# The odd layer's out projection: three quarters by seven block products, mixers as the stationary operand, residual token-major

## The chip, the cores and the metric

One Trainium2 chip; the kernel runs on one core. The metric is the device time of one execution in microseconds (us), median of the runs shown; the profile is one execution taken by the hardware profiler.

## What is computed

A trunk of two residual layers over 16 meta tokens and 256 tokens, width 2048. The odd layer (16 heads, 256 mixer channels a head) is differential attention, gated, with an out projection of 4096 by 2048, and the final norm follows:

```python
def odd_mixer(h, w_in, w_out, lam_vecs, c_norm, layer_idx):
    z = jnp.einsum('bld,de->ble', h, w_in)
    cq, ck, cv, cg = split_cols(z, (C_WIDTH, C_WIDTH, C_WIDTH, C_WIDTH))
    ...
    o = diff_attention(q, k, v, lam)
    o = rms_norm(o, c_norm) * (1.0 - lam_init)
    o = o.transpose(0, 2, 1, 3).reshape(Bn, L, C_WIDTH) * jax.nn.silu(cg)
    return jnp.einsum('ble,ed->bld', o, w_out)
...
h = h + odd_mixer(rms_norm(h, norm_c[i]), w_in_c[i], w_out_c[i], diff_lambda[i], diff_norm[i], layer)
return rms_norm(h, final_norm)[:, N_META:]
```

## The kernel before

Every large product is made of three TensorE products: each float32 operand is split into a high part (rounded to fp32r by a copy on ScalarE, L290) and a low part (the difference, on VectorE, L291); high by high, high by low and low by high are summed in PSUM.

Weights come in units of 128 x 2048 floats (1 MB): SyncE loads one into a ring of three buffers (`wr`, L301), `half` splits each half of 1024 columns into `wh` and `wl`, which are rings of four buffers each (`ws`). `run` (L313) walks a plan of units and prepares one unit ahead of the one it multiplies. A projection unit of the odd layer is 48 products into one of three `pj` banks, with the 128 x 128 weight blocks stationary and the 256 or 272 tokens moving; `out_unit` (L716) is twice 24 products and adds each result to the transposed residual `hT` (L725).

A head of the odd layer is eight projection units (q, q, k, k, v, v, g, g), and its attention (`scores_c`, `chain_c`) is started as generators that are stepped once in every 16 products (`product`, L281). Scores go into the two `sc` banks, transposes and the norm's sums into the two `tr` banks, the head's output into the `o` bank. `chain_c` ends by splitting the head's 256 channels into the mixer tiles `mh` and `ml` (L910, L912).

Four heads make a quarter of the 4096 mixer channels. From head 4 on, two out units of the quarter before stand at the end of each head (L926): 24 units for three quarters. The last quarter is multiplied in `final` with the mixers stationary and 512 weight columns moving; there the residual is first transposed into token-major `ht` (32 transposes, L942, and eight copies, L943), added up and normalized.

The order of instructions on each engine is made by a scheduler that lists the whole program by its own estimate of times; the order in the text of the kernel gives the dependences.

Of the kernel before, what the change touches and what calls it, by code (L numbers as in the profile page):

```python
# [16 lines left out]
P = 128  # L17
# [13 lines left out]
LAM_INIT = 0.8 - 0.6 * math.exp(-0.3)  # L31
BIG = -1e30
LEV = (1, 2, 4, 8, 16, 32, 64)
DIAG = len(LEV)
# [66 lines left out]
class Trunk:  # L101
# [39 lines left out]
    def setup(self):  # L141
# [37 lines left out]
        nc.vector.memset(self.kT, 0.0)  # L179
        self.qT = c.tile([P, 3 * NM + T], F32, tag="qT", name="qT")  # L180
        self.ones = c.tile([P, P], F32, tag="ones", name="ones")
        nc.vector.memset(self.ones, 1.0)
        nc.vector.tensor_copy(self.onesr, self.ones)

# [96 lines left out]
    def product(self, *args, **kw):  # L281
        if self.products == 16:
            self.products = 0
            self.tick()
        self.nc.tensor.matmul(*args, **kw)  # L285
        self.products += 1


# [19 lines left out]
    def weights(self, src, pieces=1):  # L308

        raw = self.load(src, pieces)  # L310
        return [self.half(raw, 0), self.half(raw, 1)]

    def run(self, plan):  # L313

        srcs = [u for u in plan if isinstance(u, tuple)]
        ready = {}

        def prepare(i):
            if i < len(srcs) and i not in ready:
                ready[i] = self.weights(srcs[i][0], 1 if i else 2)  # L320
# [130 lines left out]
    def chain_a(self, s, mix, slot):  # L451
# [5 lines left out]

        MT = self.one("X3", [3, L])

# [25 lines left out]
        def operands(m):  # L485
            n = (L if m <= 8 else T) // (2 * m)
            w = n * 2 * m
            i = LEV.index(m)
            KS, QS = self.one(f"ks{i % 4}", [L]), self.one(f"u{i % 2}_{i // 2 % 2}", [L])
            for dst, src in ((KS, K), (QS, Q)):  # L490
                nc.scalar.copy(  # L491
                    dst[:, :w].rearrange("p (b d m) -> p b d m", d=2, m=m), view(src, 0, [[2 * m, n], [L + m, 2], [1, m]])
                )
            if m <= 8:
                nc.gpsimd.tensor_copy(self.kT[:, 32 * i - 32 : 32 * i - 32 + NM], KS[:, T:L])
                nc.gpsimd.tensor_copy(self.qT[:, i * NM - NM : i * NM], QS[:, T:L])
            return KS, QS
# [40 lines left out]
        QT = self.two("gate", [NM])  # L538
        nc.vector.tensor_scalar(self.qT[:, 3 * NM + P :], Q[:, 0, :P], tots[:, 1, 1:2], None, op0=ALU.mult)
# [3 lines left out]
        nc.gpsimd.tensor_copy(self.qT[:, 3 * NM : 3 * NM + P], Q[:, 0, P:T])  # L543
        yield
# [7 lines left out]
        W = P + NM  # L552
        mm(tail[:, : 3 * NM + T], lhsT=self.kT, rhs=self.qT, start=True, stop=True)
        mm(xp[:, W + P : 2 * W], lhsT=K[:, 0, P:T], rhs=QT, start=True, stop=True)
# [161 lines left out]
    def out_unit(self, w, key, u, lo=0):  # L716
# [10 lines left out]
        return w[key[1] * 8 + u], products  # L727

    def in_units(self, w, base, begin, lows):
# [73 lines left out]

    def head_c(self, h, mix, slot):
        nc = self.nc
# [33 lines left out]
        def gate(j):  # L839
            def done(ps):  # L840
                if j == 0:
                    s["g"] = self.one("gC", [2, T])
                self.silu(s["g"][:, j], self.scaled(self.two("zg", [T]), ps, NM), T)
                nc.gpsimd.tensor_scalar(s["g"][:, j], s["g"][:, j], self.dn[:, j : j + 1], None, op0=ALU.mult)
                if j == 1:
                    self.start(self.chain_c(s, mix, slot))

            return done
# [3 lines left out]
    def scores_c(self, h, s):  # L852
# [37 lines left out]

    def chain_c(self, s, mix, slot):
        nc, v, wT, gC = self.nc, s["v"], s["w"], s["g"]
# [15 lines left out]
        for j in range(2):  # L908
            nc.gpsimd.tensor_tensor(gC[:, j], gC[:, j], r[:, :T], op=ALU.mult)
        nc.vector.tensor_tensor(gC, o.rearrange("p (a b) -> p a b", a=2), gC, op=ALU.mult)  # L910
        for j in range(2):
            self.split(mix[0][:, slot + j, :T], mix[1][:, slot + j, :T], gC[:, j])  # L912

    def odd(self):
        w_in, w_out = self.ins["w_in_c"], self.ins["w_out_c"]

        def head(h):
            if h % 4 == 0:
                self.mix[1, h // 4] = self.new_mix()
            return self.head_c(h, self.mix[1, h // 4], (h % 4) * 2)  # L920

        plan = [self.setup_odd, lambda: self.stats(self.prenorm(self.gc))]
        for h in range(HC):
            plan += self.in_units(w_in, 8 * h, lambda h=h: head(h), [NM, NM, 0, 0, 0, 0, NM, NM])
            if h >= 4:
                plan += [self.out_unit(w_out, (1, h // 4 - 1), (h % 4) * 2 + u, NM) for u in range(2)]  # L926
        return plan


    def final(self):  # L930
        nc, w, mix = self.nc, self.ins["w_out_c"], self.mix[1, 3]
        fb = self.big.tile([P, D], F32, tag="hl", name="fnorm")
        nc.sync.dma_start(fb, self.ins["fnorm"].broadcast_to([P, D]))
        ht = self.big.tile([P, 2, D], F32, tag="hh", name="ht")
        ms = self.const.tile([P, 2, 5], F32, tag="fms", name="fms")
        rs = self.const.tile([P, 2], F32, tag="frs", name="frs")
        for c in range(4):
            for t in range(2):
                ps = self.ps("tr")
                for e in range(4):  # L940
                    x = self.hT[:, 4 * c + e, NM + t * P : NM + t * P + P]
                    nc.tensor.transpose(ps[:, e * P : e * P + P], x, self.ident)  # L942
                nc.scalar.copy(ht[:, t, c * 512 : c * 512 + 512], ps)  # L943

        def part(ps, t, k, hi, lo, cols=slice(0, 512)):
            ts = slice(t * P, t * P + P)
            for i in range(2):
                s = slice(i * 512 + cols.start, i * 512 + cols.stop)
                kk = 2 * k + i
                last = self.three(ps[:, cols], (mix[0][:, kk, ts], mix[1][:, kk, ts]), (hi[:, s], lo[:, s]), kk == 0, kk == 7)  # L950
            return last
# [54 lines left out]
def layout(inputs):  # L1006
# [12 lines left out]
    w = f["w_out_c"][0]  # L1019
    w3 = w[: 24 * P].reshape(3, 8, P, 8, 2, P).transpose(0, 3, 2, 4, 1, 5).reshape(24, P, 2048)  # L1020
    w1 = w[24 * P :].reshape(2, 4, P, 4, 512).transpose(3, 0, 2, 1, 4).reshape(8, P, 2048)
# [32 lines left out]
```

## Time and profile before

| | |
|---|---|
| median of 3 runs | 2095.29 us (2094.68 to 2095.52) |
| the profiled execution's own time | 2095.99 us |
| its span, first to last instruction | 2094.2 us |
| TensorE busy | 2077.2 us (99%) |
| VectorE / ScalarE / GpSimd busy | 1383.5 / 1162.2 / 585.2 us (66 / 55 / 28%) |
| mean granted TensorE clock | 0.997 |

TensorE issues one instruction after the other and is the engine to look at first; the other engines prepare its operands and empty its banks. Products overlap in the pipeline, so the pace of TensorE is read from the distance between starts, not from the duration of one product.

### The profile page before, as it was taken

The page shows a single profiled execution, that of the slowest core. Times are in us where ns is not written, and L with a number is a line of the kernel's source. Part 1 is how long each engine was busy: PE and PEld are TensorE (multiplying, and loading weights), DVE is VectorE, ACT ScalarE, POOL GpSimd, SP SyncE. Part 2 cuts the span into 40 slices and gives each one's busy share as a digit, 9 for nine tenths or more (in the row PEclk, how much of TensorE's full clock was granted, in tenths as well). Part 3 has the DMA queues.
Part 4 walks back from the last instruction along what each step waited for, and adds up shares of the span by engine and source line. Part 5 has one row for each costly group of instructions (what it writes and reads, how often), then busy time and mean ns, then how long its engine had stood idle before and what let it go on. Part 6 is the DMA issues. An engine that isn't in the chain of part 4 may idle for free.

```text
span 2094.2 us, 40530 instructions
## 1 busy us (share of the span) xinstructions
PE 2077.2 (99%) x16552; PEld 2054.6 (98%) x16552; DVE 1383.5 (66%) x2440; ACT 1162.2 (55%) x2079; POOL 585.2 (28%) x631
## 2 busy tenths in 40 slices
PE   8999999999999999999999999999999999999998
PEld 8999999999999999999999999999999999999997
DVE  7888787877786666656675666665655665655654
ACT  6677666666654545445455555555445555445554
POOL 3453534433442120221022222222122222122211
PEclk9999999999999999999999999999999999999999
DMA  7344443443444444444554444444444444444453
GB/s 269 123 141 148 152 143 142 158 145 142 161 143 161 143 160 155 160 149 151 177 174 168 162 161 162 165 168 172 163 174 168 164 166 174 163 172 171 163 185 116
DMA packets 49146, 336.73 MB, mean 161 GB/s; under 512 B 5568, under 2 KB 5568, under 8 KB 9280
## 3 DMA queue, kind: packets, MB, share of 16 engines
q1 hardware_dynamic: 48240, 333.05, 45.0%
q8 instruction: 130, 2.13, 0.4%
q10 hardware_dynamic: 720, 1.09, 0.2%
q14 instruction: 56, 0.46, 0.1%
HBM read 332.03 MB, written 2.10 MB: 160 GB/s over the span
## 4 chain that ended last, share of the span: by engine, by line
PE 97%; DVE 1%; ACT 1%; issue 0%; DMA 0%; POOL 0%; SPq 0%; DVEq 0%; POOLq 0%; ACTq 0%
PE pspj L285 84%; PE pssc L502 2%; PE pstr L368 1%; PE pso L336 1%; PE pso L335 1%; PE pso L334 1%; PE pspj L334 1%; PE pspj L335 1%; PE pspj L336 1%; PE pssc L336 1%; PE pssc L334 1%; PE pssc L335 1%; PE pssc L514 1%; PE pstr L696 1%; PE pstr L887 1%; DVE wl L291 0%
## 5 line engine op out<-in xcount | busy, mean ns | idle before, releaser
L285 PE MATMUL pspj<-hl,wh 128*128 128x272 f32 (+1 forms) x3936 | 1010.5, 289 | 0.0
L285 PE MATMUL pspj<-hh,wh 128*128 128x272 f32 (+1 forms) x3936 | 1007.5, 287 | 0.0
L290 ACT CAST wh<-wr 128x1024 fp32r<-128x1024 f32 (+1 forms) x628 | 655.0, 1043 | 595.3 <-PE pspj L285 528.3
L291 DVE TENSOR_TENSOR wl<-wr,wh 128x1024 fp32r<-128x1024 f32 (+1 forms) x628 | 774.0, 1233 | 248.9 <-ACT wh L290 246.4
L285 PEld LDWEIGHTS pspj<-hl,wh 128*128 128x128 f32 x3936 | 743.0, 189 | 1.6
L285 PEld LDWEIGHTS pspj<-hh,wh 128*128 128x128 f32 x3936 | 741.1, 188 | 0.7
L285 PE MATMUL pspj<-hh,wl 128*128 128x272 f32 (+1 forms) x3936 | 573.7, 287 | 0.0
L285 PEld LDWEIGHTS pspj<-hh,wl 128*128 128x128 f32 x3936 | 519.7, 189 | 0.9
L285 PE MATMUL pspj<-mh,wh 128*128 128x272 f32 (+1 forms) x896 | 229.5, 288 | 0.0
L285 PE MATMUL pspj<-ml,wh 128*128 128x272 f32 (+1 forms) x896 | 228.9, 287 | 0.0
L285 PEld LDWEIGHTS pspj<-mh,wh 128*128 128x128 f32 x896 | 168.8, 188 | 0.5
L285 PEld LDWEIGHTS pspj<-ml,wh 128*128 128x128 f32 x896 | 169.2, 189 | 0.1
L291 POOL TENSOR_TENSOR X<-z,X 128x256 fp32r<-128x256 f32 (+1 forms) x64 | 77.1, 1206 | 325.4 <-ACT X L290 325.4
L355 DVE TENSOR_TENSOR z<-pspj,rstd 128x272 f32<-128x272 f32 (+1 forms) x114 | 49.6, 436 | 161.5 <-PE pspj L285 161.5
L725 DVE TENSOR_TENSOR hT<-hT,pspj 128x272 f32<-128x272 f32 (+1 forms) x112 | 48.1, 430 | 128.5 <-PE pspj L285 128.4
L285 PE MATMUL pspj<-mh,wl 128*128 128x272 f32 (+1 forms) x896 | 127.8, 285 | 0.0
L285 PEld LDWEIGHTS pspj<-mh,wl 128*128 128x128 f32 x896 | 116.7, 189 | 0.1
L592 POOL TENSOR_TENSOR gC<-sg,zg 128x256 f32<-128x256 f32 x32 | 23.5, 735 | 229.2 <-ACT sg L591 229.2
L856 POOL TENSOR_SCALAR X<-cf 128x272 f32<-128x272 f32 x32 | 43.4, 1365 | 117.6 <-DVE nmx L867 113.9
L423 POOL TENSOR_SCALAR X<-X,lb,lb 128x272 f32<-128x272 f32 x32 | 29.2, 911 | 131.3 <-ACT X L420 121.8
L491 ACT COPY u<-X 128x272 f32<-128x272 f32 (+1 forms) x96 | 40.1, 418 | 45.3 <-DVE X L477 43.8
L463 DVE COPY_PREDICATED X<-masks,pssc 128x256 f32<-128x256 uint8 x128 | 56.5, 441 | 2.3 <-PE pssc L502 1.7
(218 smaller groups left out, 2351.5 us busy)
## 6 DMA issues: line engine op xcount, KB each, us to landing
wr<-in_w_in_c_dram SPq DMA_DIRECT2D x128, 1024.0 KB, 4.8
wr<-in_w_in_a_dram SPq DMA_DIRECT2D x117, 1024.0 KB, 4.8
wr<-in_w_out_a_dram SPq DMA_DIRECT2D x32, 1024.0 KB, 4.9
wr<-in_w_out_c_dram SPq DMA_DIRECT2D x32, 1024.0 KB, 4.8
hT<-in_hT_dram SPq DMA_DIRECT2D x8, 272.0 KB, 6.1
wr<-in_w_in_a_dram SPq DMA_DIRECT2D x8, 256.0 KB, 6.0
wr<-in_w_in_a_dram SPq DMA_DIRECT2D x2, 512.0 KB, 6.7
fnorm<-in_fnorm_dram SPq DMA_DIRECT2D x1, 1024.0 KB, 4.6
```

Source lines behind the costliest of these rows:

```text
L285: self.nc.tensor.matmul(*args, **kw)
L290: self.nc.scalar.copy(hi, src)
L291: (low or self.nc.vector).tensor_tensor(lo, src, hi.bitcast(F32), op=ALU.subtract)
L334: mm(ps, lhsT=a[0], rhs=b[0], start=first, stop=False)
L335: mm(ps, lhsT=a[0], rhs=b[1], start=False, stop=False)
L336: return mm(ps, lhsT=a[1], rhs=b[0], start=False, stop=last)
L355: self.nc.vector.tensor_tensor(dst, ps[:, : L - lo_tok], self.rstd[:, lo_tok:], op=ALU.mult)
L463: nc.vector.copy_predicated(dst, self.masks[:, i, :].unsqueeze(1).broadcast_to([P, 2, P]), src)
L491: nc.scalar.copy(dst[:, :w].rearrange("p (b d m) -> p b d m", d=2, m=m), view(src, 0, [[2 * m, n], [L + m, 2], [1, m]]))
L502: last = mm(lp[:, c], lhsT=KS[:, c], rhs=QS[:, c], start=True, stop=True)
L725: self.nc.vector.tensor_tensor(d, d, ps[:, :n], op=ALU.add)
L856: nc.gpsimd.tensor_scalar(bias[:, i, :], self.negC[i], SLOPES[h] * RS, None, op0=ALU.mult)
```

## The change

For the first three quarters the out projection is made in `group`, in four groups of 512 output columns a quarter. The tokens (two blocks of 128), the quarter's channels (two blocks of 512) and the group's columns (two blocks of 256) form 2 x 2 blocks, and seven block products replace eight. A group takes two weight units, and of each `sums` makes four stationary-side partners on the weight side: one half as it is, two sums of 1024 columns together, one sum of 512, and one half that is partly a sum; all are split into high and low. The mixers are stationary (128 channels x 128 tokens), 256 weight columns move: 84 products a group. The products collect in two `pj` banks (`12`, `34`) and two `sc` banks (`57`, `6`) and are added to the residual at the group's end.

`chain_c` writes the mixers and, for the second two heads of a quarter, four differences of them, into fixed places (`side`). The residual is made token-major once, in the first head of the odd layer (`token_major_residual`), instead of in `final`. The four groups of a quarter stand at the end of heads 4, 8 and 12, after the second k unit and at the end of heads 5, 9 and 13, and after the second k unit of heads 6, 10 and 14. Scores use the `tr` banks. Some buffers of the even layer share places (`ks`, `qT`, `ones`) to make room for `ht`.

```diff
+    def sums(self, src):
+        raw = self.load(src)
+        t = self.spare[:, : 3 * 512]
+        a = self.half(raw, 1)
+        nc.vector.tensor_tensor(
+            t[:, :1024].rearrange("p (a b) -> p a b", a=2),
+            raw[:, :512].unsqueeze(1).broadcast_to([P, 2, 512]),
+            raw[:, 1024:].rearrange("p (a b) -> p a b", a=2),
+            op=ALU.add,
+        )
+        b = self.half(t, 0)
+        nc.vector.tensor_tensor(t[:, 1024:], t[:, :512], raw[:, 1536:], op=ALU.add)
+        c = self.parts()
+        self.split(c[0][:, :512], c[1][:, :512], t[:, 1024:])
+        nc.vector.tensor_tensor(raw[:, :512], t[:, 1024:], raw[:, 512:1024], op=ALU.add)
+        return a, b, c, self.half(raw, 0)
...
+    def group(self, w, q, g):
+        def products(hp, ws):
+            if hp == 0:
+                acc["12"], acc["34"] = self.ps("pj"), self.ps("pj")
+                acc["57"], acc["6"] = self.ps("sc"), self.ps("sc")
+            for part, order in enumerate(
+                ((("X11", "12", 0), ("s3", "34", 0)), (("s1", "57", 0), ("s7", "57", 1)), (("s6", "6", 0),), (("X22", "34", 1), ("X12", "12", 1)))
+            ):
...
+                        for i, (a, b) in enumerate(((xh, wh), (xh, wl), (xl, wh))):
...
+            x = self.two("z", [256])
+            nc.scalar.copy(x, acc["6"][:, :256])
+            nc.vector.tensor_tensor(x, x, p1, op=ALU.subtract)
+            zy = self.spare[:, 3584:4096]
+            nc.vector.tensor_tensor(pair(zy), pair(acc["57"]), x.unsqueeze(1).broadcast_to([P, 2, 256]), op=ALU.add)
...
+            add(h22, acc["57"][:, :256])
+            add(h11, p1)
+            add(h11, p2)
+            add(view(ht, c0 + 256, [[D - 256, 2], [1, 256]]), pair(acc["34"]))
+            add(view(ht, c0 + 256, [[D, 2], [1, 256]]), pair(zy))
+            add(h21, zy[:, 256:], ALU.subtract)
...
-                ps = self.ps("sc")
+                ps = self.ps("tr")
                 c = slice(i * P, i * P + P)
                 self.three(ps[:, :L], (q[:, j, 0, c], q[:, j, 1, c]), (k[:, j, 0], k[:, j, 1]), True, True)
...
-        nc.vector.tensor_tensor(gC, o.rearrange("p (a b) -> p a b", a=2), gC, op=ALU.mult)
-        for j in range(2):
-            self.split(mix[0][:, slot + j, :T], mix[1][:, slot + j, :T], gC[:, j])
...
+        if not half:
+            put("X11", X1[:, :, :P])
+            return
+        put("X12", X[:, :, :P])
+        put("X22", X[:, :, P:])
+        if q == 3:
+            put("X21", X1[:, :, P:])
+            return
+        S = self.spare[:, 2560:3584].rearrange("p (a b c) -> p a b c", a=4, b=2)
+        for i, a, b in ((0, X1[:, :, P:], X[:, :, P:]), (2, X1[:, :, P:], X1[:, :, :P]), (1, X1[:, :, :P], S[:, 0]), (3, X[:, :, :P], S[:, 1])):
+            nc.vector.tensor_tensor(S[:, i], a, b, op=ALU.subtract)
+        for i in range(4):
+            put(SIDES[i], S[:, i])
...
-            if h >= 4:
-                plan += [self.out_unit(w_out, (1, h // 4 - 1), (h % 4) * 2 + u, NM) for u in range(2)]
+            g = {0: [0], 1: [1, 2], 2: [3]}.get(h % 4, []) if h >= 4 else []
+            for i in g:
+                at = 5 if i in (1, 3) else len(units)
+                units[at:at] = self.group(w_out, h // 4 - 1, i)
```

The first place in the order of instructions is VectorE at an out projection. Before, around the two out units that end head 4 (`hT` is the residual, `wl` a low part, `gC` the head's output, `zg` an emptied gate unit):

```order
L355 TENSOR_TENSOR zg_2487_16521<-pspj_2486_16472,rstd_2064_13441 128x256 [waits PE_49]
L291 TENSOR_TENSOR wl_2493_16536<-wr_2489_16529,wh_2492_16535 128x1024 [waits DVE_49,Activation_49]
L725 TENSOR_TENSOR hT_94<-hT_94,pspj_2494_16539 128x256 [waits PE_49]
L291 TENSOR_TENSOR wl_2503_16628<-wr_2501_16625,wh_2502_16627 128x1024 [waits DMAHW5_49,DVE_49,Activation_49]
L725 TENSOR_TENSOR hT_94<-hT_94,pspj_2498_16586 128x256 [waits PE_49]
L291 TENSOR_TENSOR wl_2505_16632<-wr_2501_16625,wh_2504_16631 128x1024 [waits DVE_49,Activation_49]
L725 TENSOR_TENSOR hT_94<-hT_94,pspj_2506_16635 128x256 [waits PE_49]
```

and now, on VectorE at the end of the group that stands inside head 5 (`pspj_2584` is bank `12`, `pspj_2585` bank `34`, `pssc_2586` bank `57`; `u`, `dd`, `nmx` belong to the head's softmax; `wl_2597` to `wl_2614` are the low parts of the two v units that follow):

```order
L967 TENSOR_SCALAR u1_0_2594_17118<-u1_0_2594_17118,dd_2590_17107 128x272 [waits DVE_49]
L291 TENSOR_TENSOR wl_2599_17148<-wr_2595_17141,wh_2598_17147 128x1024 [waits Activation_49]
L968 SCALAR_TENSOR_TENSOR u0_0_2592_17112<-u0_0_2592_17112,dd_2590_17107,u1_0_2594_17118 128x272 [waits DVE_49]
L795 TENSOR_TENSOR ht_13473<-ht_13473,pspj_2585_17072 128x2x256 [waits PE_49]
L792 TENSOR_TENSOR z_2609_17228<-z_2609_17228,pspj_2584_17071 128x256 [waits PE_49,Activation_49]
L795 TENSOR_TENSOR ht_13473<-ht_13473,pspj_2584_17071 128x256
L291 TENSOR_TENSOR wl_2612_17241<-wr_2610_17238,wh_2611_17240 128x1024 [waits DMAHW4_49,Activation_49]
L965 RECIPROCAL dd_2601_17154<-dd_2601_17154 128x2 [waits Activation_49]
L794 TENSOR_TENSOR spare_13681<-pssc_2586_17073,z_2609_17228 128x512 [waits DVE_49]
L795 TENSOR_TENSOR ht_13473<-ht_13473,pssc_2586_17073 128x256
L291 TENSOR_TENSOR wl_2614_17245<-wr_2610_17238,wh_2613_17244 128x1024 [waits Activation_49]
L795 TENSOR_TENSOR ht_13473<-ht_13473,pspj_2584_17071 128x256 [waits DVE_49]
```

The one addition per bank has become a row of steps between the splits for the next units, and the last read of bank `12` comes last of them.

TensorE meets this at the second v unit, whose bank is the one that held `12`:

```order
L286 MATMUL pspj_2615_17248<-hl_2074_13407,wh_2598_17147 128x272
L286 MATMUL pspj_2615_17248<-hh_2073_13406,wl_2599_17148 128x272 x8
L286 MATMUL pspj_2623_17310<-hh_2073_13406,wh_2611_17240 128x272 [waits DVE_49,Activation_49]
L286 MATMUL pspj_2623_17310<-hl_2074_13407,wh_2611_17240 128x272
L286 MATMUL pspj_2623_17310<-hh_2073_13406,wh_2611_17240 128x272
```

The wait on VectorE in the third row is for that last read.

The second place is TensorE after the last projection unit of head 15 (`pso` collects the head's output). Before, an out unit follows between its products:

```order
L336 MATMUL pso_3588_24761<-X3_3559_24549,X4_3551_24519 128x256
L285 MATMUL pspj_3587_24760<-mh_2805_18928,wh_3575_24685 128x256
L285 MATMUL pspj_3587_24760<-ml_2806_18929,wh_3575_24685 128x256
L285 MATMUL pspj_3587_24760<-mh_2805_18928,wh_3575_24685 128x256
L285 MATMUL pspj_3587_24760<-ml_2806_18929,wh_3575_24685 128x256
```

and now the final quarter's products:

```order
L355 MATMUL pso_3719_25174<-X3_3701_24983,X4_3693_24953 128x256
L353 MATMUL pspj_3734_25234<-wh_3725_25216,mh_2083_13460 128x512
L354 MATMUL pspj_3734_25234<-wl_3726_25217,mh_2083_13460 128x512
L355 MATMUL pspj_3734_25234<-wh_3725_25216,ml_2084_13461 128x512
L353 MATMUL pspj_3734_25234<-wh_3725_25216,mh_2083_13460 128x512
```

The two out units that stood behind the last head are gone from there; the products of the final quarter that need the last head's mixers are put behind 56 others that do not.

## Rows read from the trace of the kernel before

**Rows 1.** The page: busy time of TensorE and of the slices, and the chain.
```profile
PE 2077.2 (99%) x16552; PEld 2054.6 (98%) x16552; DVE 1383.5 (66%) x2440; ACT 1162.2 (55%) x2079; POOL 585.2 (28%) x631
...
PE 97%; DVE 1%; ACT 1%; issue 0%; DMA 0%; POOL 0%; SPq 0%; DVEq 0%; POOLq 0%; ACTq 0%
```

**Rows 2.** Windows of the odd layer, then last 8.4 us: busy us (instructions), clock, DMA.
```profile
core 0: us, PE busy (x) PEld busy (x) DVE busy (x) ACT busy (x) POOL busy (x), PEclk, DMA share, GB/s
1125.00:1331.00 206.00, 206.00 (x1697) 205.69 (x1697) 124.76 (x205) 111.55 (x197) 57.80 (x56) 1.00 0.47 164
1345.00:1595.00 250.00, 250.00 (x2070) 249.69 (x2069) 146.20 (x236) 128.58 (x212) 58.40 (x55) 1.00 0.48 167
...
2085.80:2094.20 8.40, 0.28 (x3) 0.08 (x1) 2.12 (x5) 1.73 (x5) 0.00 (x0) 0.64 0.52 178
```

**Rows 3.** Timeline of VectorE (start us, us, what): one step of each head.
```profile
1190.76 0.68 DVE L910 TENSOR_TENSOR gC<-pso,gC 128x512 f32<-128x512 f32 x1
1242.28 0.68 DVE L910 TENSOR_TENSOR gC<-pso,gC 128x512 f32<-128x512 f32 x1
...
1408.22 0.68 DVE L910 TENSOR_TENSOR gC<-pso,gC 128x512 f32<-128x512 f32 x1
1471.11 0.68 DVE L910 TENSOR_TENSOR gC<-pso,gC 128x512 f32<-128x512 f32 x1
```

**Rows 4.** Timeline of TensorE: products with the mixers stationary, 512 and 256 wide.
```profile
2080.02 0.39 PE L336 MATMUL pspj<-wh,ml 128*128 128x512 f32 x1
2080.25 0.28 PE L334 MATMUL pspj<-wh,mh 128*128 128x256 f32 x1
...
2085.80 0.28 PE L336 MATMUL pssc<-wh,ml 128*128 128x256 f32 x1
```

**Rows 5.** Timeline of TensorE: same group of a projection unit, 24 products apart.
```profile
1193.48 1.16 PE L285 MATMUL pspj<-hh,wl 128*128 128x272 f32 x8
1196.50 1.16 PE L285 MATMUL pspj<-hh,wl 128*128 128x272 f32 x8
```

**Rows 6.** The final's transposes, in the chain that ended last.
```profile
2037.97 0.87 PE pstr L942 x8
```

**Rows 7.** Groups of VectorE by form, 1345 to 1845 us (busy us, mean ns, idle before).
```profile
L291 DVE TENSOR_TENSOR wl<-wr,wh 128x1024 fp32r<-128x1024 f32 x160 | 198.5, 1241 | 72.1 <-ACT wh L290 72.1
L725 DVE TENSOR_TENSOR hT<-hT,pspj 128x256 f32<-128x256 f32 x31 | 13.1, 422 | 46.2 <-PE pspj L285 46.2
...
L291 DVE TENSOR_TENSOR X<-pstr,X 128x512 fp32r<-128x512 f32 x8 | 5.5, 684 | 0.0
L910 DVE TENSOR_TENSOR gC<-pso,gC 128x512 f32<-128x512 f32 x8 | 5.4, 678 | 0.0
```

**Rows 8.** The same window on ScalarE.
```profile
L290 ACT CAST wh<-wr 128x1024 fp32r<-128x1024 f32 x159 | 166.9, 1050 | 192.0 <-PE pspj L285 174.3 <-issue 17.7
```

**Rows 9.** Timeline around the last head's chain, all engines but TensorE.
```profile
2027.15 0.60 ACT L901 ACTIVATE X<-pso 128x512 f32<-128x512 f32 x1 [0.61 <-PE pso L899]
...
2029.62 1.22 DVE L291 TENSOR_TENSOR wl<-wr,wh 128x1024 fp32r<-128x1024 f32 x1
2029.77 1.66 POOL L291 TENSOR_TENSOR X<-X,X 128x256 fp32r<-128x256 f32 x1 [0.68 <-ACT X L290]
...
2034.64 1.45 POOL L909 TENSOR_TENSOR gC<-gC,u 128x256 f32<-128x256 f32 x2 [3.21 <-ACT u L391]
...
2035.62 1.54 DVE L291 TENSOR_TENSOR wl<-wr,wh 128x1024 fp32r<-128x1024 f32 x1
...
2039.48 0.75 DVE L291 TENSOR_TENSOR ml<-gC,mh 128x256 fp32r<-128x256 f32 x2
```

**Rows 10.** What TensorE waited for in the whole run (us, times, longest).
```profile
PE pssc L285 <- DVE hl L240: 3.4, 2, 1.8
...
PE pssc L285 <- DVE wl L291: 1.7, 1, 1.7
PE pssc L502 <- DVE X L466: 1.1, 1, 1.1
```

More of the change, by code (lines that the diff above doesn't have):

```diff
@@ L319, in prepare @@
             if i < len(srcs) and i not in ready:
-                ready[i] = self.weights(srcs[i][0], 1 if i else 2)
+                ready[i] = srcs[i][2](srcs[i][0]) if len(srcs[i]) > 2 else self.weights(srcs[i][0], 1 if i else 2)
         i = 0
@@ L456, in chain_a @@
         yield
[L458 removed]
+        MT, qT = self.one("X3", [3, L]), self.one("u_2", [3 * NM + T])
         def keep(i, lp):
@@ L727, in out_unit, with side @@
         return w[key[1] * 8 + u], products
+    def side(self, kind, p, n=1, q=0):
+        b, off = (q % 2, 0) if kind == "X11" else ((q + 1) % 2, 0) if kind == "X21" else divmod(SIDES.index(kind), 3)
+        off = p * P + (0 if kind in ("X11", "X21") else 512 + off * 512)
+        return [x[:, off : off + n * P] for x in self.cm[b]]
+    def group(self, w, q, g):
+        nc, acc = self.nc, {}
+        def products(hp, ws):
[5 more added lines that the diff above has]
+            ):
+                for pr in range(2):
+                    for e, (kind, bank, half) in enumerate(order):
+                        xh, xl = self.side(kind, 2 * hp + pr, 1, q)
+                        e = half if kind in ("s1", "s7") else {"X11": 0, "s3": 1, "s6": 0, "X22": 0, "X12": 1}[kind]
+                        c = slice(e * 512 + pr * 256, e * 512 + pr * 256 + 256)
+                        wh, wl = ws[part][0][:, c], ws[part][1][:, c]
+                        ps = acc[bank][:, half * 256 : half * 256 + 256]
+                        first, last = hp + pr == 0, hp + pr == 2
+                        for i, (a, b) in enumerate(((xh, wh), (xh, wl), (xl, wh))):
+                            start = first and i == 0
+                            with self.tc.issue_after(acc["first" + bank]) if start and half else nullcontext():
+                                ins = self.product(ps, lhsT=a, rhs=b, start=start and not half, stop=last and i == 2, skip_group_check=True)
+                            if start and not half:
+                                acc["first" + bank] = ins.ins
+            if hp == 0:
+                return
+            ht, c0 = self.ht, g * 512
+            p1, p2 = acc["12"][:, :256], acc["12"][:, 256:]
+            pair = lambda x: x.rearrange("p (a b) -> p a b", a=2)
+            x = self.two("z", [256])
[3 more added lines that the diff above has]
+            nc.vector.tensor_tensor(pair(zy), pair(acc["57"]), x.unsqueeze(1).broadcast_to([P, 2, 256]), op=ALU.add)
+            add = lambda d, a, op=ALU.add: nc.vector.tensor_tensor(d, d, a, op=op)
+            h11, h21, h22 = ht[:, 0, c0 : c0 + 256], ht[:, 1, c0 : c0 + 256], ht[:, 1, c0 + 256 : c0 + 512]
+            add(h22, acc["57"][:, :256])
[4 more added lines that the diff above has]
+            add(h21, zy[:, 256:], ALU.subtract)
+        return [(w[(q * 4 + g) * 2 + hp], lambda ws, hp=hp: products(hp, ws), self.sums) for hp in range(2)]
@@ new lines, in token_major_residual @@
+    def token_major_residual(self):
+        nc = self.nc
+        self.ht = self.big.tile([P, 2, D], F32, tag="ht", name="ht")
+        for c in range(4):
+            for t in range(2):
+                yield
+                ps = self.ps("tr")
+                for e in range(4):
+                    x = self.hT[:, 4 * c + e, NM + t * P : NM + t * P + P]
+                    nc.tensor.transpose(ps[:, e * P : e * P + P], x, self.ident)
+                nc.scalar.copy(self.ht[:, t, c * 512 : c * 512 + 512], ps)
+        self.spare = self.big.tile([P, NJ * L], F32, tag="hT", name="spare")
@@ L914, in odd, with first @@
+        for i in range(4):
+            put(SIDES[i], S[:, i])
     def odd(self):
         w_in, w_out = self.ins["w_in_c"], self.ins["w_out_c"]
[L917 to L922, printed above, removed]
-        for h in range(HC):
-            plan += self.in_units(w_in, 8 * h, lambda h=h: head(h), [NM, NM, 0, 0, 0, 0, NM, NM])
-            if h >= 4:
-                plan += [self.out_unit(w_out, (1, h // 4 - 1), (h % 4) * 2 + u, NM) for u in range(2)]
+        def first():
+            self.cm = [self.new_mix() for _ in range(2)]
+            self.cm = [[x.rearrange("p a b -> p (a b)") for x in m] for m in self.cm]
+            self.start(self.token_major_residual())
```

58 lines of the change are left out of this document (33 added, 25 removed).

## Prediction

> **What bounds the kernel.** I read the page first: TensorE is busy 99% of the span and makes 97% of the chain that ended last [rows 1]. The windows then show where that holds: in the odd layer TensorE is busy in every microsecond at full clock, while VectorE has 124.76 of 206 us of work and GpSimd less [rows 2]. The list of waits names the first products of the program and one wait of 1.1 us in the even layer [rows 10]: nowhere in the odd layer does TensorE wait by a measurable amount. So time there is the number of products times the distance between their starts, as long as the other engines stay ahead. The last 8.4 us hold three products [rows 2]; that tail (last additions, norm, stores) is left as it is.
>
> Two prices follow. A head without out units lasts 1242.28 - 1190.76 = 51.52 us, one with two lasts 1471.11 - 1408.22 = 62.89 us [rows 3]: two out units, 96 products, are 11.37 us of pure TensorE time. And products of just the kind the change uses (mixers stationary, 256 columns moving) stand at the end of the program: 48 of them, 47 distances in 2085.80 - 2080.25 = 5.55 us, so 0.1181 us each [rows 4].
>
> **The change, part by part.**
>
> *Products.* Three quarters of eight out units become 12 groups of 84 products. A group costs 84 x 0.1181 = 9.92 us against 11.37: 1.45 us less, 12 times, **-17.4 us**. By 144 products fewer at 0.1181 it would be -17.0. All of it is on the path that sets the end.
>
> *The transposes* leave the final part and enter the first head of the odd layer. Eight took 0.87 us [rows 6], so 32 are 3.5 us, taken away in one full stretch of TensorE and added in another: **0**. Their eight copies on ScalarE run beside a first head in which ScalarE has 111.55 of 206 us of work [rows 2].
>
> *Weight sums and splits.* For one group VectorE has six low parts of 1024 (1.241 us), two of 512 (0.684), two sums of 1024 (taken as a low part, 1.22, [rows 9]), four of 512 (0.678), and at the end five steps of 256 (0.422) and three of 512 [rows 7]: 7.45 + 1.37 + 2.44 + 2.71 + 2.11 + 2.03 = 18.1 us. Two out units had 4 x 1.241 + 4 x 0.422 = 6.7 us. So VectorE gets 11.4 us more in a stretch that gets shorter. Steps that follow each other overlap a little (two low parts of 256, each of the 0.42 us of a step that size, took 0.75 us together [rows 7, 9]: 0.09 us), over some 20 steps 1.8 us, so 16.3 to 18.1 us. The groups stand half a head apart: 51.52 / 2 + 9.92 = 35.7 us of TensorE, in which VectorE has half of a head's 31.2 us (124.76 / 4) and one group: 31.9 to 33.7 us, **89 to 94%** against some 60% now. That still fits, but with 2 to 4 us to spare in each cycle, the attention not evenly spread. ScalarE gets 7.5 casts of 1024 instead of four and a small copy [rows 8], 4 us more on 19 (111.55 / 206 x 35.7) in such a cycle: it has room. The mixers' differences and extra splits (8 subtractions, 6 splits of 256 a quarter) are some 6 us a quarter, spread over heads by the scheduler; in the cycles that have them VectorE comes to 95%.
>
> So I walked through the orders at the group inside head 5, with time 0 at its first product and 0.07 us of overlap taken off each VectorE step. Its last weight part can only be cast when the last part of the unit before is used up, at 5.7; ScalarE is done at 6.75, VectorE at 7.9, TensorE needs it at 10.0: no wait. Then come two score steps (the second can start at 8.6, when TensorE has made it), three splits, the softmax steps and the additions in the order shown; from 9.1 on these are 8.5 us, so bank `12` is free at **17.6**. TensorE is through with the group and the 12 score products between at 11.4, with the next unit (48 at (1196.50 - 1193.48) / 24 = 0.126, [rows 5]) and two transposes at **17.7**, and then needs that bank. That is a tie: without the overlap VectorE is 1.1 us late. The same walk at the group that ends a head (no scores) leaves 1 to 2 us. I take 0.5 us for each of the six groups inside a head and nothing for the others: **+3 us**. The lower end is 0 (TensorE never waits now). The upper is 13 us: all 12 groups late by the 1.1 us.
>
> *The moved load queue.* The weight loads are the same 32; a sum unit holds its buffer until its last split, at 7.9 us after the group's start, and what is loaded into it is first needed at about 18; a load of 10 us would still be in time. Nothing; without that distance the unit two behind would be late.
>
> *The program's end.* The last head's chain loses the two out units that stood behind it. In the trace it takes from 2027.1 to 2040.2, about 13 us [rows 9], with its norm issued late among out products. Now its norm sums stand behind 30 products of 512 at 0.23 us [rows 4], 7 us after the head's last product, and the mixers are ready at 11.4 (high) and 11.9 (low); TensorE has 20 more such products and arrives at 11.9 and 12.4. **+0.5 us**, from 0 to 2.
>
> *Everything else* (shared buffers in the even layer, a memset less, scores in the `tr` banks) changes when steps are issued, not their number. TensorE had no waits there and the even layer's VectorE share does not change: 0, give or take 1 us.
>
> Sum: -17.4 + 3 + 0.5 = -13.9 us. The profiled execution took 2095.99 us, so 2082.1 by it; it lies 0.7 above the median, so I say **2081.5** for the median.
>
> *A rule against the change.* In the trace a low part took 1.54 us instead of 1.22 while GpSimd ran two additions [rows 9], and another GpSimd step took 1.66 us beside a low part. By the Trainium skill (SBUF - State Buffer, "Who interferes with whom") that is what happens when a VectorE step with two SBUF inputs meets a GpSimd step that reads SBUF: one blocks the other for the whole instruction. The trace agrees. All the added sums and splits are such steps; by the mean of the low parts [rows 7] the sum gets nothing for it, and by the rule at every step it becomes the first rival.
>
> **Rivals.**
>
> *The lock makes VectorE the bound (slower).* Of the 18 us a group, some 17 steps have both inputs in SBUF. GpSimd is busy 58.4 of 250 us, 23% [rows 2]. If a meeting costs 0.32 us as in the row, chance meetings are 17 x 0.23 x 0.32 = 1.3 us a group; if every one met and paid it, 5.4 us, and a cycle would need 33.7 + 5.4 = 39 us against 35.7: 3.4 us lost in each, 41 us in all, 2119. It decides from where VectorE's delay passes its slack by 1.45 us a group, which eats the whole gain; at 1.8 us the time is over 2099.5. Against it: the mean low part is 1241 ns beside a bare 1.22 [rows 7, 9], so meetings cost 0.02 us on average. Chance 6%.
>
> *VectorE is late in every cycle.* In-order waits, on scores above all, leave holes in an engine that is 90 to 95% full. At 0.7 to 1.1 us for each of 12 groups: 8 to 13 us lost, 2087 to 2092. For it: the walk's tie; against it: what is late in one cycle is caught up in the four units that follow. Chance 20%; with 1.1 to 1.8 us a group, no measurable change, another 9%.
>
> *The sums don't reach TensorE at all in time, or the products run slower than those at the end.* Two half banks filled in turn are not in the trace; the final part alternates whole banks without a gap. With 0.123 us a product the gain would be 12.5 instead of 17.4, 2086. Chance 5%, inside the range.
>
> **How the numbers follow.** The forecast case (0 to 8 us lost) has 60% and gives 2077 to 2086. With the late cycles and the slower products the range is **2077 to 2092**, which leaves some 15% above and a little below. A measurement of this kernel can tell about 0.2%, 4.2 us. Faster by that is below 2091.1: 60 + 5 + 18 of the late cycles, **0.83**. Within it 0.11; slower 0.06.
>
> **What would show it.** Right: TensorE instructions fewer by 144; group products 0.118 us apart; VectorE busy 130 to 155 us more; TensorE waits in the odd layer few, and those on VectorE steps of the residual (bank `12`) or on low parts, a few us in all; the tail still 8.4 us. Wrong: waits of 1.5 us or more at each group; low parts with a mean well over 1.24 us and GpSimd steps beside them; a gap before the last head's mixers in the final part; or a distance over 0.12 us between group products.

## The result, and the profile after

The changed kernel takes 2081.32 us (median of 4 runs, 2081.09 to 2082.60) against 2095.12 us (4 runs, 2094.68 to 2095.52) of the kernel before on the same chip: 13.8 us less, ratio 0.9935, 95% interval 0.9918 to 0.9953. The prediction was 2081.5. The profiled execution took 2081.48 us, its span is 2079.7 us against 2094.2, 14.5 us less; the terms below are held against that.

The page of the changed kernel: span, busy time, VectorE's 40 slices, and the chain that ended last.

```profile
span 2079.7 us, 40519 instructions
...
PE 2063.0 (99%) x16408; PEld 2039.4 (98%) x16408; DVE 1533.0 (74%) x2650; ACT 1204.0 (58%) x2157; POOL 608.6 (29%) x631
...
DVE  8888887887676656656575666798768896688854
...
PE 92%; DVE 3%; ACT 2%; POOL 1%; issue 1%; DMA 1%; SPq 0%; DVEq 0%; ACTq 0%; POOLq 0%
```

Beside [rows 1]: 144 products fewer (16552 to 16408), VectorE up 149.5 us (1383.5 to 1533.0), and higher slices of VectorE in the last third, where the groups lie. TensorE is still the engine that is always busy.

What TensorE waited for in the whole run of the changed kernel (us in all, times, longest):

```profile
PE pstr L175 <- DVE wS L170: 2.1, 1, 2.1
PE pssc L286 <- DVE hl L240: 2.1, 2, 1.8
PE pssc L286 <- DVE wl L291: 1.7, 1, 1.7
PE pssc L521 <- ACT u L510: 1.0, 2, 0.6
PE pspj L353 <- ACT mh L290: 0.5, 1, 0.5
PE pssc L533 <- POOL X L525: 0.5, 2, 0.3
PE pssc L286 <- ACT hh L239: 0.4, 1, 0.4
```

One line is of the odd layer, the one on `mh`: 0.5 us in the final part, on the last head's mixers. At the twelve groups there is no wait. L521 and L533 are the scan of the even layer, in the first 250 us; beside [rows 10] they are new, or stand in place of the 1.1 us there.

Windows of the changed kernel from the end of one group to the end of the next, three cycles of the first quarter (busy us and instructions of TensorE, its weight loads, VectorE, ScalarE, GpSimd; clock, DMA):

```profile
1348.95:1383.92 34.97, 34.97 (x291) 34.97 (x290) 31.55 (x51) 19.22 (x28) 9.84 (x7) 1.00 0.54 193
1383.92:1420.60 36.68, 36.68 (x306) 36.60 (x305) 32.23 (x46) 23.82 (x41) 9.94 (x10) 1.00 0.48 166
1420.60:1455.53 34.93, 34.93 (x291) 34.93 (x289) 31.72 (x50) 19.20 (x30) 10.14 (x7) 1.00 0.53 186
```

VectorE works 88 to 91% of a cycle, at full TensorE clock and with TensorE busy throughout.

**Where the time went.** The two products on the sink row in each head's attention make a mark. Timeline of TensorE, first mark of heads 0, 3, 7 and 15 in the changed kernel, then of heads 0 and 15 in the kernel before:

```profile
1132.47 0.28 PE L990 MATMUL pso<-wS,vS 80*128 80x256 f32 x1
...
1286.99 0.28 PE L990 MATMUL pso<-wS,vS 80*128 80x256 f32 x1
...
1533.34 0.28 PE L990 MATMUL pso<-wS,vS 80*128 80x256 f32 x1
...
2026.72 0.28 PE L990 MATMUL pso<-wS,vS 80*128 80x256 f32 x1
```

```profile
1128.12 0.28 PE L899 MATMUL pso<-wS,vS 80*128 80x256 f32 x1
...
2025.98 0.28 PE L899 MATMUL pso<-wS,vS 80*128 80x256 f32 x1
```

- Head 0 comes 4.35 us later: about 3.5 us are the 32 transposes, the rest, 0.85 us, is there before the odd layer begins (see the run of the even layer's edits below).
- Four heads with four groups take 1533.34 - 1286.99 = 246.35 us. A head without a group takes 51.51 us in this trace too, so a group costs (246.35 - 4 x 51.51) / 4 = **10.08 us**, 0.1200 us a product, where the prediction had 9.92. Two out units cost 11.37 [rows 3]: 12 x (11.37 - 10.08) = 15.5 us gained, not 17.4.
- From the mark of head 15 to the end: 52.98 us against 68.22, 15.24 less. The two out units that stood there (11.37) and the transposes (3.5) make 14.9 of it; the remaining 0.4 is what three final products ahead of the mark (0.68) and somewhat faster products of 512 columns (below) give, less the wait of 0.5 us and what else moved there.

### The profile page after: what moved, and what is told of

Same layout as the page of the kernel before. It is cut to its first block, busy times and chain, and to the rows that moved or that the text cites. A ratio compares the mean times of both kernels' runs of the same rounds, so it can differ in the third digit from the quotient of the medians.

```text
span 2079.7 us, 40519 instructions
## 1 busy us (share of the span) xinstructions
PE 2063.0 (99%) x16408; PEld 2039.4 (98%) x16408; DVE 1533.0 (74%) x2650; ACT 1204.0 (58%) x2157; POOL 608.6 (29%) x631
## 4 chain that ended last, share of the span: by engine, by line
PE 92%; DVE 3%; ACT 2%; POOL 1%; issue 1%; DMA 1%; SPq 0%; DVEq 0%; ACTq 0%; POOLq 0%
PE pspj L286 78%; PE pssc L286 3%; PE pssc L521 2%; DVE wl L291 1%; PE pstr L387 1%; PE pso L355 1%; PE pso L354 1%; ACT wh L290 1%; PE pso L353 1%; PE pssc L533 1%; DMA wr<-in_w_in_a_dram 1%; PE pspj L353 1%; PE pstr L715 1%; PE pspj L355 1%; PE pspj L354 1%
## 5 line engine op out<-in xcount | busy, mean ns | idle before, releaser
L291 DVE TENSOR_TENSOR wl<-wr,wh 128x1024 fp32r<-128x1024 f32 (+1 forms) x628 | 777.0, 1239 | 217.0 <-ACT wh L290 205.1
L291 POOL TENSOR_TENSOR X<-z,X 128x256 fp32r<-128x256 f32 (+1 forms) x64 | 84.0, 1313 | 256.7 <-ACT X L290 256.7
L286 PE MATMUL pspj<-mh,wh 128*128 128x272 f32 x512 | 135.0, 293 | 0.0
L286 PE MATMUL pspj<-ml,wh 128*128 128x272 f32 x512 | 134.5, 291 | 0.0
L510 ACT COPY u<-X 128x272 f32<-128x272 f32 (+1 forms) x192 | 78.3, 417 | 86.7 <-DVE X L496 50.3
L286 PEld LDWEIGHTS pspj<-mh,wh 128*128 128x128 f32 x512 | 96.3, 188 | 0.5
L286 PEld LDWEIGHTS pspj<-ml,wh 128*128 128x128 f32 x512 | 96.5, 189 | 0.1
L286 PE MATMUL pspj<-mh,wl 128*128 128x272 f32 x512 | 74.8, 288 | 0.0
L744 DVE TENSOR_TENSOR hT<-hT,pspj 128x272 f32<-128x272 f32 x64 | 27.9, 436 | 57.0 <-PE pspj L286 57.0
L286 PEld LDWEIGHTS pspj<-mh,wl 128*128 128x128 f32 x512 | 68.1, 188 | 0.1
```

The costliest lines, as they stand in the source:

```text
L286: return self.nc.tensor.matmul(*args, **kw)
L291: (low or self.nc.vector).tensor_tensor(lo, src, hi.bitcast(F32), op=ALU.subtract)
L510: nc.scalar.copy(dst[:, :w].rearrange("p (b d m) -> p b d m", d=2, m=m), view(src, 0, [[2 * m, n], [L + m, 2], [1, m]]))
```

## The experiments

All times are medians beside the kernel before on the same chip, which took 2094.88 to 2095.26 us. "A quarter" is the distance from the mark of head 3 to that of head 7, four heads with four groups: 246.35 us in the changed kernel.

**Eight products, in the new form.** The groups are kept, without sums; each line of the new table is a mixer block, a bank, its half, and which of the two weight blocks of the part:

```
-    return a, b, c, self.half(raw, 0)
+    return self.half(raw, 1), self.half(raw, 0)
...
-    ((("X11", "12", 0), ("s3", "34", 0)), (("s1", "57", 0), ("s7", "57", 1)), (("s6", "6", 0),), (("X22", "34", 1), ("X12", "12", 1)))
+    (("X11", "1", 0, 0), ("X21", "2", 0, 0), ("X12", "1", 1, 1), ("X22", "2", 1, 1)),
+    (("X12", "1", 0, 1), ("X22", "2", 0, 1), ("X11", "1", 1, 0), ("X21", "2", 1, 0)),
...
```

> The changed kernel with eight plain block products a group in place of seven: mixers stationary, residual token-major, transposes early, as in the change, but no sums of weights, no differences of mixers, and two additions of 512 columns to the residual a group. Theory (TensorE is the bound, VectorE's added steps cost nothing): 144 products more at the 0.120 us that the groups of the changed kernel show, +17.3 us, 2098.6 us (2097 to 2100); a cycle with a group 1.44 us longer. Rival (the seven products' VectorE steps cost TensorE time that no wait shows): less than +16 us.

Measured: 2098.45 us (2098.16 to 2099.91), ratio 1.0017 (1.0008 to 1.0026). A quarter is 252.08 us, a group 11.51, 1.43 more than with seven. The 144 products are worth 17.1 us, and all the sums and differences on VectorE cost TensorE nothing. It also shows that the rest of the change (token-major, mixers stationary) is by itself a loss, 3.6 us: 96 products take 11.51 us this way and took 11.37 in the two out units, 1.7 us over 12 groups. The other 1.9 us were not taken apart; the even layer's edits account for some 0.2 of them (below).

**Where the stationary blocks lie.** Group products stand 0.1200 us apart; the prediction's 0.1181 came from the same kind of product, with the mixers elsewhere in their tile.

```
-    off = p * P + (0 if kind in ("X11", "X21") else 512 + off * 512)
+    off = (p + (0 if kind in ("X11", "X21") else 4 + off * 4)) * 136
...
```

> The changed kernel with its mixer blocks 136 elements apart in place of 128, as blocks of the kernel before lay (272 for two); nothing else. Theory (the distance of 0.120 in place of 0.118 us between group products comes from where the stationary blocks lie): 1008 group products at 0.118, -1.9 us, and the 168 products of 512 columns of the final part back from 0.227 to 0.232 us, +0.8: 2080.2 us, a group 9.92 us. Rival (the distance has another cause): 2081.3, a group 10.08 us.

Measured: 2080.29 us (2079.83 to 2080.80). A quarter is 245.81 us, so a group 9.94. Timeline of TensorE in the changed kernel, and with the stride of 136, two starts 12 products apart in the first group:

```profile
1340.21 0.28 PE L286 MATMUL pssc<-wh,mh 128*128 128x256 f32 x1
...
1341.65 0.28 PE L286 MATMUL pssc<-wh,mh 128*128 128x256 f32 x1
```

```profile
1339.57 0.28 PE L286 MATMUL pssc<-wh,mh 128*128 128x256 f32 x1
...
1340.99 0.28 PE L286 MATMUL pssc<-wh,mh 128*128 128x256 f32 x1
```

1.44 us against 1.42: 0.1200 and 0.1183 each. In the final part the 512 columns went the other way, 0.2275 to 0.2322 on average.

> The changed kernel with all its mixer blocks moved by 8 elements (32 bytes), still 128 elements apart. It tells apart what in the stride mattered. If the place of each block counts (128 elements apart puts every block on a multiple of 512 bytes, 136 apart does not): group products at 0.118, products of 512 columns at 0.232, as with the stride of 136, 2080 to 2081. If the distance between blocks counts: 0.120 and 0.227 as in the changed kernel, 2081.3.

Its edit is `+ 8` at the end of the line that the stride's edit takes out. Measured: 2080.53 us (2080.49 to 2080.69), a quarter 245.90 us, 0.1186 us for 256 columns and 0.2332 us for 512. So the place of each block counts, not the distance between blocks: with every block on a multiple of 512 bytes from the start of its tile, 256 columns take 0.120 and 512 take 0.227; away from it 0.118 to 0.119 and 0.232 to 0.233. Why is not shown. The weight loads of the group products have a mean of 190 to 191 ns in the changed kernel and 188 with the stride of 136, which would fit a longer load; but those of the 512 columns have 188 ns in both, so the length of the load does not explain their distance. By the Trainium skill (TensorE: Matmul & The Clock Gate, "Back-to-back issue gap") the distance in a stream of such pairs is set by the load and the product together; the rows of 256 columns fit, those of 512 show no change of the load, and it says nothing of places.

**The tie at bank `12`.** The prediction's 3 us of waits rest on it. Changed kernel, VectorE's steps on the banks and TensorE around them, after the first group inside head 5 (first product at 1372.49):

```profile
1383.92 0.28 PE L286 MATMUL pspj<-wh,ml 128*128 128x256 f32 x1
1384.04 0.29 PE L286 MATMUL pspj<-hh,wh 128*128 128x272 f32 x1
1385.38 0.67 DVE L795 TENSOR_TENSOR ht<-ht,pspj 128x512 f32<-128x512 f32 x1
1385.97 0.41 DVE L792 TENSOR_TENSOR z<-z,pspj 128x256 f32<-128x256 f32 x1
1386.30 0.41 DVE L795 TENSOR_TENSOR ht<-ht,pspj 128x256 f32<-128x256 f32 x1
...
1389.90 0.40 DVE L795 TENSOR_TENSOR ht<-ht,pspj 128x256 f32<-128x256 f32 x1
1390.29 0.29 PE L286 MATMUL pspj<-hh,wh 128*128 128x272 f32 x1
```

The group ends at 1384.04, 11.55 us after its first product (walked: 11.4). The last read of bank `12` starts at 1389.90 and ends at 1390.30, 17.8 us after the first product (walked: 17.6), and the second unit starts at 1390.29, at 17.80 (walked: 17.7). By the times this looks like the forecast tie, without a wait. To tell a lucky tie from a wrong bank, one step was put in front of that read:

```
     add(h11, p1)
+    add(x, p1)
     add(h11, p2)
```

> The changed kernel with one more VectorE addition of 256 columns (0.41 us, into a scratch tile, the output is the same) before the last read of bank 12 in each group. It also lets one more low part past that read. Theory (the tie of the prediction is real: after the first group inside a head, VectorE's last read of bank 12 ends within 0.1 us of TensorE's need): that read comes about 1.6 us later there, 3 waits of 1.6 us; after the second group inside a head it comes 3.2 us later against a distance of some 2 us, 3 waits of 1.2; none at the ends of heads: +8 us, 2089.5 us, each wait on that addition. Rival (there is slack that the trace does not show, or the next wait is made up): 2081 to 2083.

Measured: 2081.36 us (2081.26 to 2081.53), no change. In this kernel:

```profile
1390.27 0.29 PE L286 MATMUL pspj<-hh,wh 128*128 128x272 f32 x1
1391.14 0.40 DVE L795 TENSOR_TENSOR z<-z,pspj 128x256 f32<-128x256 f32 x1
1391.46 0.41 DVE L795 TENSOR_TENSOR ht<-ht,pspj 128x256 f32<-128x256 f32 x1
```

The unit starts 1.6 us before the last read of bank `12` ends, so it does not write there. The changed kernel's own trace says the same at the group that ends at 1455.53, the second one inside a head:

```profile
1461.92 0.29 PE L286 MATMUL pspj<-hh,wh 128*128 128x272 f32 x1
1462.48 0.41 DVE L795 TENSOR_TENSOR ht<-ht,pspj 128x256 f32<-128x256 f32 x1
```

The second unit starts there 0.97 us before that read ends; it starts ahead of its end, by 0.01 to 0.98 us, after 9 of the 12 groups. So the section on the change has this wrong: the second v unit's bank is not the one that held `12`, and its wait on VectorE in the order is not for that read. The bank of `34` had been read by 1386.05 (the step of 512 at 1385.38 above) and was there to be had. My theory fell; its replacement, that units get whichever bank came free first, was tried with six steps in place of one:

> The changed kernel with six more VectorE additions of 256 columns before the last read of bank 12, which then comes some 20 us after the group. Theory (units are given whichever bank of the three was released first, so two banks carry the units as long as they are read at once, and bank 12 is only missed when the next group wants two, 25 us later): 2081 to 2084. Rival (a unit behind the group does take bank 12 in its turn, with a few us of room): that unit waits more than 10 us in each of 6 groups, over 2140.

Measured: 2081.21 us (2081.00 to 2081.38). The last read now ends at 1404.38, 20.5 us after the group's last product, and TensorE has no wait in the odd layer but the 0.5 us of the final part. In this kernel bank `12` is read 14 us behind the second unit's start and costs nothing: there is no tie. That banks go by the order in which they come free fits all this, but no row names the bank of a unit.

**How full may VectorE be?** Six such steps behind all others, and in the second kernel `range(16)`:

```
     add(h21, zy[:, 256:], ALU.subtract)
+    for _ in range(6):
+        add(x, h21)
```

> The changed kernel with six more VectorE additions of 256 columns a group (some 0.35 us each, 2.1 us a group, 25 us in all, into a scratch tile, the output is the same) behind the last step of the residual, so that bank 12 is not read later. Theory (the amount of VectorE work does not matter while it is not full, only what stands before a step that TensorE needs): VectorE 95 to 98% busy in a cycle with a group, 0 to +3 us, 2081 to 2084. Rival (VectorE is full enough that its work comes through one to one): 1.5 to 2.1 us for each of 12 groups, +18 to +25 us, 2099 to 2106.

Measured: 2081.74 us (2081.02 to 2082.68), a quarter 246.34 us as without them. In the cycles whose windows stand above, VectorE works 34.05 of 34.97, 34.04 of 36.68 and 33.95 of 34.93 us, 93 to 97%, and TensorE does not wait in them.

> The changed kernel with sixteen more VectorE additions of 256 columns a group (0.34 us each, 5.4 us a group) behind the last step of the residual, into a scratch tile. VectorE has 31.97 us of work in a cycle of 35.53 in the changed kernel, so it would have 37.4. Theory (work on VectorE is free up to the length of the cycle and costs one to one beyond it): 1.9 us late in each of the three cycles between the groups of a quarter, made up in the stretch without groups, 9 times 1.9, +17 us, 2098 (2088 to 2105), with waits of TensorE on low parts or on the residual. Rival (the order hides it, the added steps slide behind everything TensorE needs): under 2085.

Measured: 2107.10 us (2105.70 to 2109.35), ratio 1.0057 (1.0042 to 1.0072): slower than before, and 9 us more than forecast. The waits are on what was said (TensorE waited 9.5 us for low parts and 2.3 for casts), with one of 3.0 to 3.2 us in each quarter in place of three of 1.9, but they are not the whole price. Windows of this kernel inside the first quarter (columns as above), the last four of them as one, then one of the changed kernel with about as many products, then TensorE's timeline after the longest wait there:

```profile
1430.00:1435.00 5.00, 5.00 (x43) 5.00 (x43) 4.80 (x7) 2.43 (x4) 3.50 (x1) 1.00 0.57 210
1435.00:1440.00 5.00, 3.88 (x29) 3.46 (x28) 3.86 (x8) 2.03 (x3) 1.10 (x2) 1.00 0.60 210
1440.00:1445.00 5.00, 2.70 (x11) 2.40 (x11) 4.46 (x9) 0.45 (x2) 0.00 (x0) 0.71 0.00 0
1445.00:1450.00 5.00, 4.18 (x17) 3.89 (x18) 4.36 (x11) 1.93 (x3) 1.96 (x1) 0.50 0.00 0
1450.00:1455.00 5.00, 5.00 (x33) 5.00 (x33) 4.90 (x9) 1.82 (x4) 2.11 (x2) 0.77 0.49 165
1435.00:1455.00 20.00, 15.76 (x88) 14.75 (x88) 17.59 (x34) 6.23 (x11) 5.17 (x5) 0.74 0.27 94
```

```profile
1434.00:1445.00 11.00, 11.00 (x90) 11.00 (x90) 9.31 (x12) 4.62 (x7) 2.71 (x2) 1.00 0.28 97
```

```profile
1442.03 0.56 PE L286 MATMUL pssc<-wl,mh 128*128 128x256 f32 x1 [3.01 <-DVE wl L291]
...
1443.24 0.41 PE L286 MATMUL pssc<-wh,mh 128*128 128x256 f32 x1
...
1443.88 0.41 PE L286 MATMUL pssc<-wh,mh 128*128 128x256 f32 x1
```

After a wait of 3.01 us the granted clock is 0.50, 1.2 of 2.4 GHz, and products stand 0.21 us apart ((1443.88 - 1443.24) / 3) in place of 0.12, until it is back at 1.00 some 10 us later. The 88 products of the 20 us from 1435 to 1455 take the changed kernel some 11 us. So 9 us are lost in this stretch: TensorE is idle for 4.24 of them, and the rest goes with the slower products. Here the waits cost their own time and about as much again. The three quarters lost 10.0, 7.8 and 8.4 us against the changed kernel.

**VectorE's steps beside GpSimd's.** Eight GpSimd additions of 256 columns a group, into a scratch tile:

```
     add(h21, zy[:, 256:], ALU.subtract)
+    for i in range(8):
+        nc.gpsimd.tensor_tensor(self.spare[:, 4096:], h21, h11, op=ALU.add)
```

> The changed kernel with eight more GpSimd additions of 256 columns a group into a scratch tile, some 10 us a group: GpSimd 20 us busy in a cycle of 35.5 in place of 9.9. Theory (a meeting of the two engines lengthens the GpSimd step far more than the VectorE step): low parts with a mean below 1.27 us, the GpSimd additions above 1.2 us, 2081 to 2083. Rival (every meeting blocks VectorE for a whole GpSimd step or at the 0.32 us of the row of before): VectorE gets 2 us a cycle or more, is full at 35 us of 35.5, low parts with a mean over 1.35 us beside the groups, 2085 to 2100.

Measured: 2092.03 us (2090.44 to 2092.74), 10.7 us lost: the time and the low parts are those of the rival. Groups of VectorE from 1350 to 1460 us (three groups), by form, in the changed kernel and then in this one, where GpSimd's additions stand in the second row:

```profile
L291 DVE TENSOR_TENSOR wl<-wr,wh 128x1024 fp32r<-128x1024 f32 x37 | 45.7, 1239 | 6.3 <-ACT wh L290 6.3
...
L319 DVE TENSOR_TENSOR spare<-wr 128x1024 f32<-128x1024 f32 x6 | 8.2, 1370 | 0.1
...
L329 DVE TENSOR_TENSOR wr<-spare,wr 128x512 f32<-128x512 f32 x6 | 4.7, 777 | 0.1
```

```profile
L291 DVE TENSOR_TENSOR wl<-wr,wh 128x1024 fp32r<-128x1024 f32 x35 | 47.3, 1354 | 2.3 <-ACT wh L290 2.1
...
L804 POOL TENSOR_TENSOR spare<-ht 128x256 f32<-128x256 f32 x24 | 33.5, 1395 | 13.3 <-DVE ht L795 11.8
L319 DVE TENSOR_TENSOR spare<-wr 128x1024 f32<-128x1024 f32 x6 | 9.3, 1549 | 0.1
...
L329 DVE TENSOR_TENSOR wr<-spare,wr 128x512 f32<-128x512 f32 x6 | 6.2, 1034 | 0.1
```

A low part goes from 1239 to 1354 ns, a sum of 512 from 777 to 1034. Over the forms with two inputs in SBUF (low parts, the three sums, the low parts of sums) that is 35 x 0.115 + 6 x (0.179 + 0.153 + 0.349 + 0.257 + 0.125), some 10 us for 24 GpSimd additions, 0.43 us for each. VectorE then has no room left, 49.49 us of work from 1350 to 1400. The Trainium skill's rule (SBUF - State Buffer, "Who interferes with whom"), that such a pair of steps locks one out, agrees in kind; the trace gives 0.43 us on VectorE for a GpSimd step of 1.4. TensorE's named waits are on GpSimd's split of the score inputs, which stands behind the added steps (4.7 us), and on VectorE (1.6 us): how much of the 10.7 us is the lock and how much that queue, this run does not tell apart, nor that a full VectorE is what sets the time.

**The even layer's edits alone**, on the kernel before:

```
-    nc.vector.memset(self.ones, 1.0)
...
+    self.ones = self.onesr.bitcast(F32)
...
-    MT = self.one("X3", [3, L])
+    MT, qT = self.one("X3", [3, L]), self.one("u_2", [3 * NM + T])
...
-    KS, QS = self.one(f"ks{i % 4}", [L]), self.one(f"u{i % 2}_{i // 2 % 2}", [L])
+    KS, QS = self.one(f"u{2 + i % 2}_{i // 2 % 2}", [L]), self.one(f"u{i % 2}_{i // 2 % 2}", [L])
...
```

> The kernel before with the change's edits of the even layer alone: the scan's key and query buffers under shared tags, the table of ones taken from the other one. Theory (0.8 us of the change's gain is given back there: in the trace of the changed kernel the even layer's products are 0.8 us later from 310 us on, with two new waits of TensorE of 1.0 and 0.5 us in the first 250 us): the same two waits, heads of the odd layer 0.8 us later, 2095.7 us (2095.3 to 2096.3). Rival (those 0.8 us are chance of that execution's start, or come from the odd layer's edits): the head's marks where they were, 2094.9.

Measured: 2096.40 us (2096.25 to 2096.61) against 2095.05, ratio 1.0006 (0.9996 to 1.0015): a little above the range, and not told apart from the kernel before. Its list of waits has the two new ones, and head 0's mark is 0.61 us later than in the kernel before:

```profile
PE pssc L501 <- ACT u L490: 0.9, 2, 0.6
PE pssc L513 <- POOL X L505: 0.5, 2, 0.3
```

But most of that is there before the two waits, the first of which ends at 128 us. The first product on `wS` and `vS` in the even layer, in the kernel before, in this one and in the changed one:

```profile
79.30 0.29 PE L573 MATMUL pso<-wS,vS 80*128 80x272 f32 x1
79.71 0.29 PE L572 MATMUL pso<-wS,vS 80*128 80x272 f32 x1
79.93 0.29 PE L592 MATMUL pso<-wS,vS 80*128 80x272 f32 x1
```

It comes 0.41 us later here and 0.63 us later in the changed kernel. In the profiles of the kernels derived from the changed one it lies between 79.33 and 80.41 us, and head 0's mark between 1131.84 and 1132.92: the program's start varies by that much. From this product to head 0's mark, these edits add 0.20 us. So some 0.2 of the 0.85 us come from them, and some 0.6 from the start of that one execution; the theory's 0.8 us was too much.

**The fastest.** Stride 136 for the three quarters of the groups, 128 for the last one, whose products are 512 wide:

```
+    step = P if q == 3 else 136
+    off = (p + (0 if kind in ("X11", "X21") else 4 + off * 4)) * step
...
```

> The changed kernel with mixer blocks 136 elements apart for the three quarters that the groups use, and 128 apart for the last quarter, which the final part uses. Theory (each width has its better place: 256 columns 0.118 us at the stride of 136, 512 columns 0.227 at that of 128): 1.7 us less in the groups, the final part as in the changed kernel, 2079.6 us (2079.2 to 2080.4), the fastest of all. Rival (the 512 columns' distance does not come from the stationary blocks): 2080.3, as with one stride.

Measured: 2079.46 us (2079.35 to 2081.03), ratio 0.9926 (0.9913 to 0.9940), the fastest of all: a quarter is 245.81 us, 512 columns take 0.2275.

## Why the prediction was right, and where only its sum was

The forecast case came in: TensorE is the bound, and VectorE's added work is hidden. But three terms were off and nearly cancelled, so that 2081.5 came within 0.2 us of the measured time is luck:

| term | predicted, us | measured, us |
|---|---|---|
| 12 groups for 12 pairs of out units | -17.4 | -15.5 |
| transposes moved | 0 | +3.5 - 3.5 |
| waits at the groups | +3 | 0 |
| program's end | +0.5 | wait of 0.5, against some -0.7 from 512 columns at 0.2275 in place of 0.2318 |
| everything else | 0 +- 1 | +0.85: some 0.2 by the even layer's edits, some 0.6 by the program's start |
| sum | -13.9 | -14.9 by these terms, -14.5 by the spans |

- **Products, mis-sized by 1.9 us.** The step "products of just the kind the change uses ... so 0.1181 us each [rows 4]" took a price over from the same operation with its stationary operand at other places. By run, 0.1200 at the change's places and 0.1183 with the blocks moved; the sign "group products 0.118 us apart" did not come in. That "everything on the path" counts at full price was right: 144 products were worth 17.1 us.
- **Waits at the groups, the step that failed.** "... and then needs that bank" was the false half of a walk whose times were right to 0.2 us: the order shows when a step is issued, and I took the banks to be handed round in turn. The next unit takes another bank: it starts up to 0.98 us before the last read of `12` ends, and moving that read some 14 us behind its start cost nothing. With the right bank the walk would have given no wait, and the term 0.
- **VectorE's load, right.** 89 to 94% was forecast and 88 to 91% measured, 130 to 155 us more and 149.5 measured. It did become longer per step beside GpSimd (the sums of 1024 took a mean of 1333 ns from 1345 to 1845 us, not 1220; low parts of 512 took 907, not 684): about 0.9 us a group, where the first rival put 1.3 for chance meetings.
- **The rivals.** "VectorE late in every cycle" is false here and true 5.4 us of work a group further on. "The lock makes VectorE the bound" had a price of the right size (0.32 us a meeting, 0.43 per added GpSimd step measured); with GpSimd's 9.9 us in a cycle it did not come. At twice that, 10.7 of the 13.8 us are gone, but 4.7 of the 6.3 us that TensorE is listed as waiting there are for GpSimd's own queue, so that the lock alone does it is not shown. Nor do 0.32 and 0.43 us show a step held up for a whole GpSimd step (0.73 us, half of the 1.45 in [rows 9], and 1.4 here). "Slower products" is what happened, at 0.120 us in place of 0.123.
- **The tail** is 8.4 us as before (2079.7 less the last product's start at 2071.29).

## What to carry to other kernels

Where one engine is always busy, count its instructions at the price of their own form and place, and check the others only for being full within the cycle in which their work must fit: here VectorE could go to 97% for nothing, and beyond the cycle its work cost more than TensorE's waits for it. Before pricing a wait on a buffer, find which buffer the waiting step really gets. Terms that cancel make a right total; read each of them in the second trace.

## What was not expected of the hardware

- The distance between products depends on where the stationary block lies: 0.1200 against 0.1183 us at 256 columns, 0.2275 against 0.2322 at 512, with opposite signs (multiples of 512 bytes in the tile against other places).
- After a TensorE wait of 3.01 us the granted clock was 0.50 and came back to 1.00 some 10 us later, so that an overrun of VectorE by 5% of a cycle cost 26 us, where the listed waits on its parts and on the casts are 11.8. In the run with GpSimd's additions, where the longest wait in the odd layer is 1.23 us, it stayed at 1.00.
- One added GpSimd addition of 256 columns went with 0.43 us more, on average, in VectorE's steps with two SBUF inputs.
